# Order of the projections at the entry of a two-layer mixing stage: queries and keys by turns, and where their transposes, up projections and squares go

## The chip, the cores and the metric

The kernel runs on one core of one Trainium2 chip, in one launch. The metric is the device time of one execution in microseconds; for the kernel before it is the median of three runs. A core has a tensor engine (TensorE, PE in the profile; its weight loads are PEld), a vector engine (VectorE, DVE), a scalar engine (ScalarE, ACT), GpSimd (POOL) and SyncE (SP, which issues nearly all DMAs). Each engine works through its own instructions in order, and semaphores order them between engines.

## The reference

Two layers of a diffusion trunk, with 256 latent tokens and 256 context tokens of 1024 features. Each layer is a half-step gated feed-forward (FFN), a mixing stage and a second FFN; every sub-layer has an RMS norm with shift, scale and gate computed from the condition. The mixing stage projects the normalised tokens to five things and merges three groups of heads:

```python
q_lat, kv_lat, k_pe, sg_in, cv_in = jnp.split(hn @ w_mix_in[l], splits, axis=-1)
if last:   # layer 1: of the context only keys and values
    kv_lat_c, k_pe_c = jnp.split(hnc @ w_mix_in[l][:, OFF_KV:OFF_SG], [KV_LORA], axis=-1)
q = mla_queries(q_lat, g_q_lat[l], w_q_up[l], g_q_head[l], rope)
k, v = mla_keys_values(kv_lat, k_pe, g_kv_lat[l], w_kv_up[l], g_k_head[l], rope)
kc, vc = mla_keys_values(kv_lat_c, k_pe_c, g_kv_lat[l], w_kv_up[l], g_k_head[l], None)
attn = latent_attention(q, k, v, kc, vc)
sg = spatial_gating(sg_in, g_sgu[l], w_spatial[l], b_spatial[l])
cv = short_conv(cv_in, w_conv[l])
h = h + mod_l[5] * merge_groups(attn, sg, cv, g_out[l], w_mix_out[l])
```

Query latents have 384 columns, key and value latents 256 and the rotary part 32. Both are RMS-normalised, projected up to 8 heads, normalised again per head, and the rotary part is rotated. All is in float32.

## The kernel before

Every matrix product is three products of rounded halves: a weight block w is split into whi (rounded, by ScalarE, L124) and wlo (the rest, by VectorE or GpSimd, L125), the activations into xh and xl alike, and TensorE adds xh·whi, xl·whi and xh·wlo (`mm3` L393, `mm3x` L404 with the activations stationary).

The class `Weights` (L60) streams the weight blocks. SyncE loads them into six raw buffers, and at most five split blocks are held (`SUBB`). `pump(n)` issues the DMAs that have a buffer and splits up to n blocks that have a slot; with `W.hold` set, a plain pump splits none. `done(i)` gives a block's slot back in order. `W.low` names the engine of the low halves; the last job of an FFN sets it to GpSimd ("g", L627) and the next FFN's first job sets it to VectorE, so all low halves of a mixing stage are GpSimd's.

The program is a list of jobs, issued in order, and this order is the order of every engine's queue. TensorE's products go to six PSUM banks (`mm_bank`) and small ones to two (`sm_bank`).

At the border between two sub-layers a generator `chain` (L435) normalises the residual: squares summed by one-column products (`sums`), their inverse root (`rstd`), spread over the partitions by two products (`spread`), and then eight chunks, one per 128 features, each a VectorE multiplication (L364) into a scratch bank, a ScalarE rounding (L368) and a VectorE rest (L369). `step(c, n)` issues n such steps, `finish(c)` the rest. There is one chain for the latents (`c`) and one for the context (`cc`); both use the same two scratch banks in turn. The last block of an FFN (`out_last`) begins the latents' chain and prepares the first blocks of the mixing stage.

Mixing then runs, for layer 0 (`full`) and layer 1: `kv_lat` (L769), in which the steps of both chains alternate with the key products of the latents (288 columns) in three parts of 3, 3 and 2 k, and with half of the query products of the latents (384 columns); `kv_ctx` (L791), the keys of the context and the rest of the queries; in layer 0 `q_ctx`; `k_prep` (GpSimd's rotary tables); `uv_lat` (L869), the gate's products (512 columns), after which layer 1 transposes the normalised key and query latents (`kv_tr`, `q_tr`, L753) and normalises the gate (`v_norm`); six `conv_block`s with `spatial` behind the fourth; `y_sg`; `k_up` (L989); `y_cv_stats`; `q_up` (L1039); `y_cv`. Attention (`att`, L1229) runs the eight heads as a pipeline, beginning with the values' up projection (`v_up`). `mo_head`, `mo_block` and `mo_last` project the merged heads into the residual: `resid` (L410) adds a block (L415), squares it (L425) and adds the squares to a sum (L429), from which the next norm starts.

At the very start, `init` sums the squares of the input and `first_blocks` computes the first modulation (`ada0`, L1417) between the first FFN's products.

Of the kernel before, what the change touches and what calls it, by code (L numbers as in the profile page):

```python
# [173 lines left out]
def hybrid_trunk_kernel(ctx: ExitStack, tc: tile.TileContext, io: dict, out: bass.AP):  # L174
# [494 lines left out]
    def mixing(l):  # L669
# [99 lines left out]
        def kv_lat(W):  # L769
            c, cc = st.pop("lat_chain"), st.pop("ctx_chain")  # L770
            P["kvs"] = list(zip([W.take(), W.take(), W.take()], (3, 3, 2)))
            step(c, 2)
            b = [mm_bank(), mm_bank()]
            tok_part(b, P["kvs"][0:1], 0, 288, (0, 1))
            step(cc)
            step(c, 3)
            tok_part(b, P["kvs"][1:2], 3, 288, (0, 1))
            step(cc)
            finish(c)
            tok_part(b, P["kvs"][2:3], 6, 288, (0, 1))  # L780
            W.pump(2)
            step(cc, 3)
            qs = P["qs"] = [(W.take(), 2) for _ in range(2)]
            qb = P["qb"] = [mm_bank(), mm_bank()]
            tok_part(qb, qs, 0, 384, (0, 1))
            finish(cc)
            W.hold = False
            lat_evac(b, 256, "kvn0", (0, 1))
        job(kv_lat, kv_spec + q_spec[0:1])

        def kv_ctx(W):  # L791
# [5 lines left out]
            lat_evac(P["qb"], 384, "qn0")  # L797
            if not full:
                for (i, _, _), _ in P["qs"]:
                    W.done(i)  # L800
                preload(AF.Gelu_apprx_tanh)
        job(kv_ctx, q_spec[1:2])

# [65 lines left out]
        def uv_lat(W):  # L869
            P["uvs"] = [(W.take(), 2) for _ in range(4)]  # L870
            b = tok_mm(P["uvs"], 512, (0, 1), not full, W)
            uv_evac(b, (0, 1))
            if not full:
                kv_tr()
                q_tr()
                preload(AF.Sqrt)
                v_norm((0, 1), b)
        job(uv_lat, uv_spec)
# [110 lines left out]
        def k_up(W):  # L989
# [27 lines left out]
            last()  # L1017
            W.done(s)

        def v_up(W):  # L1020
# [18 lines left out]
        def q_up(W):  # L1039
            subs = [W.take() for _ in range(3)]  # L1040
            last = None
            for t in range(nq):
# [43 lines left out]
            last()  # L1086
            preload(AF.Exp)

        job(y_sg)
        job(k_up, ku_spec)  # L1090
        job(y_cv_stats)
        job(q_up, qu_spec)
        job(y_cv)
# [198 lines left out]
        sl = slice(0, NQ)  # L1292

        def mo_begin():
            j = len(P["mo"]) - 1
# [7 lines left out]
        def mo_head(W):  # L1303
# [15 lines left out]
            for j in range(3):  # L1319
                W.done(subs[j][0])  # L1320
                for s in halves():
                    resid(l, 5, j, banks[j], s, j == 0)
        job(mo_head)

        def mo_block(j):
            def fn(W):
# [4 lines left out]
                for hf in halves():  # L1331
                    resid(l, 5, j, bank, hf, False)
            return fn
# [3 lines left out]
        def mo_last(W):  # L1337
# [3 lines left out]
            for s, j in zip(subs, (6, 7)):  # L1341
                bl = mm_bank()
                mo_mm(bl, s, SC + AT, LAT, True, True)
                resid(l, 5, j, bl, LAT, False, last=not full and j == 7)
            if full:
# [27 lines left out]
    def init(W):  # L1373
# [25 lines left out]
        for i in range(40):  # L1399
            PE.matmul(bank[:, 128 * (i % 4):128 * (i % 4) + 128], lhsT=ones, rhs=ones, start=True, stop=True)  # L1400
        banks = [sums([acc[:, s]]) for s in (LAT, CTX)]
        st["init_rb"] = [(bank, rstd(bank, D)) for bank in banks]
    job(init)

    def first_blocks(in_spec, evac, half_mm):
# [5 lines left out]
        def ada0(W, j):  # L1411
            bank = sm_bank()
            for rnd in range(2):
# [23 lines left out]
        def fn(W):  # L1437
            rbs = st["acc"]
            W.pump(1)
            for s, (bank, r) in zip((LAT, CTX), st.pop("init_rb")):  # L1440
                ACT.activation(rbs[:, s], spread(bank, r), AF.Copy)
            bank = None
            sbs = {0: ada0(W, 0)}
            banks = [mm_bank() for _ in range(5)]
# [190 lines left out]
```

## Time and profile before

| | |
|---|---|
| median of three runs | 1722.94 us (1720.17 to 1725.0) |
| profiled execution | 1724.47 us, span 1722.7 us |
| PE, DVE, ACT, POOL busy | 97%, 66%, 39%, 14% |
| mean granted TensorE clock | 0.994 |
| DMA | 248.53 MB, mean 144 GB/s |

Times in the trace count from the start of the span. A busy TensorE share counts matmuls from start to end, and neighbours overlap; the rate of a dense stretch is read from the distance of their starts. The idle time of an engine is put down to what ended it. In the trace of this kernel layer 0's mixing stage begins at about 403 us and layer 1's at about 1370 us, and layer 1's attention at about 1451 us.

### The profile page before, as it was taken

Reading aid. Unit: us, or ns where it says so; the run is one execution under the profiler, and the core shown is the slowest. Engines: PE = TensorE matmul, PEld = TensorE weight load, DVE = VectorE, ACT = ScalarE, POOL = GpSimd, SP = SyncE. Lnnn points to the kernel's source line nnn. Section 1 sums busy time; section 2 is a strip of 40 time slices with the busy share of each in tenths; the row PEclk is TensorE's granted clock in tenths of the full one; section 3 lists DMA queues with packets and bytes.
Section 4 is the critical chain, followed back from the end, with each engine's and each line's share of the span. In section 5 each row is a group of like instructions: output and inputs, shape, how many; then the busy total and the mean of one; then the engine's idle time right before and its main releaser. Section 6 shows DMA issues by size and latency. Waiting matters only on the chain.

```text
span 1722.7 us, 23129 instructions
## 1 busy us (share of the span) xinstructions
PE 1678.1 (97%) x8858; PEld 1403.0 (81%) x8858; DVE 1140.6 (66%) x1868; ACT 668.8 (39%) x1139; POOL 246.0 (14%) x190
## 2 busy tenths in 40 slices
PE   8999999999999999999999999999999989899999
PEld 5788888888887788888878898888877877688887
DVE  5689988744257475777777447777776446577764
ACT  4422232224558543222322243322322266555552
POOL 0000000002447432000000030000000166630000
PEclk9999999999999999999999999999999999999999
DMA  8556566532321025555555325555554332146563
GB/s 310 184 184 190 190 189 191 163 105 81 95 86 50 20 92 155 164 169 162 162 167 162 119 88 159 171 171 170 156 166 147 88 115 94 50 159 190 182 189 89
DMA packets 71392, 248.53 MB, mean 144 GB/s; under 512 B 8048, under 2 KB 9584, under 8 KB 71280
## 3 DMA queue, kind: packets, MB, share of 16 engines
q1 hardware_dynamic: 71136, 246.97, 45.8%
q8 instruction: 70, 1.15, 0.3%
q14 instruction: 42, 0.34, 0.1%
q10 hardware_dynamic: 144, 0.07, 0.0%
HBM read 245.96 MB, written 1.05 MB: 143 GB/s over the span
## 4 chain that ended last, share of the span: by engine, by line
PE 89%; DVE 4%; POOL 2%; issue 2%; ACT 2%; DMA 1%; ACTq 0%; POOLq 0%; DVEq 0%
PE mm L394 23%; PE mm L395 23%; PE mm L396 22%; PE mm L401 7%; PE mm L402 4%; PE mm L405 2%; PE mm L407 2%; PE mm L406 2%; DVE acc L429 1%; POOL p L1168 1%; POOL wlo L125 1%; DVE mm L364 1%; DMA raw<-in_w_ada 1%; PE mm L1400 1%; PE mm L1188 1%
## 5 line engine op out<-in xcount | busy, mean ns | idle before, releaser
L124 ACT ACTIVATE whi<-raw 128x1024 fp32r<-128x1024 f32 (+1 forms) x334 | 340.0, 1022 | 606.8 <-PE mm L395 520.0
L394 PE MATMUL mm<-x,whi 128*128 128x512 f32 (+1 forms) x1360 | 508.4, 374 | 3.4 <-ACT x L366 2.0
L395 PE MATMUL mm<-x,whi 128*128 128x512 f32 (+1 forms) x1360 | 504.5, 371 | 2.2 <-DVE x L369 1.9
L396 PE MATMUL mm<-x,wlo 128*128 128x512 f32 (+1 forms) x1360 | 503.1, 370 | 0.5 <-DVE wlo L125 0.5
L125 DVE TENSOR_TENSOR wlo<-raw,whi 128x1024 fp32r<-128x1024 f32 (+2 forms) x257 | 304.4, 1187 | 237.1 <-ACT whi L124 236.9
L125 POOL TENSOR_TENSOR wlo<-raw,whi 128x1024 fp32r<-128x1024 f32 (+3 forms) x77 | 172.4, 2259 | 1205.0 <-ACT whi L124 1205.0
L269 DVE SCALAR_TENSOR_TENSOR scratch<-raw,cs,scratch 128x512 f32<-128x512 f32 x448 | 307.4, 745 | 0.0
L394 PEld LDWEIGHTS mm<-x,whi 128*128 128x128 f32 x1360 | 258.2, 190 | 51.3 <-issue 4.0
L395 PEld LDWEIGHTS mm<-x,whi 128*128 128x128 f32 x1360 | 258.3, 190 | 45.9 <-DVE x L369 3.8
L396 PEld LDWEIGHTS mm<-x,wlo 128*128 128x128 f32 x1360 | 258.3, 190 | 43.8 <-DVE wlo L125 0.9
L394 PE MATMUL mm<-g,whi 128*128 128x512 f32 (+1 forms) x594 | 220.9, 372 | 0.0
L396 PE MATMUL mm<-g,wlo 128*128 128x512 f32 (+1 forms) x594 | 219.4, 369 | 0.0
L395 PE MATMUL mm<-g,whi 128*128 128x512 f32 (+1 forms) x594 | 219.4, 369 | 0.0
L401 PE MATMUL mm<-x,whi 128*128 128x512 f32 x352 | 127.0, 405 | 1.8 <-DVE x L369 1.8
L395 PEld LDWEIGHTS mm<-g,whi 128*128 128x128 f32 x594 | 111.9, 188 | 20.6
L396 PEld LDWEIGHTS mm<-g,wlo 128*128 128x128 f32 x594 | 111.6, 188 | 20.9
L394 PEld LDWEIGHTS mm<-g,whi 128*128 128x128 f32 x594 | 111.7, 188 | 20.8
L487 ACT ACTIVATE g<-sa 128x512 fp32r<-128x512 f32 (+1 forms) x88 | 50.9, 579 | 130.1 <-DVE sa L478 119.3
L402 PE MATMUL mm<-x,wlo 128*128 128x256 f32 x352 | 100.0, 284 | 0.0
L488 DVE TENSOR_TENSOR g<-sa,g 128x512 fp32r<-128x512 f32 (+1 forms) x88 | 55.1, 626 | 56.8 <-ACT g L487 56.8
L401 PEld LDWEIGHTS mm<-x,whi 128*128 128x128 f32 x352 | 67.4, 192 | 18.9 <-DVE x L369 2.0
L402 PEld LDWEIGHTS mm<-x,wlo 128*128 128x128 f32 x352 | 67.9, 193 | 0.0
(218 smaller groups left out, 1777.1 us busy)
## 6 DMA issues: line engine op xcount, KB each, us to landing
raw<-in_w_ffn_in SPq DMA_DIRECT2D x176, 512.0 KB, 4.1
raw<-in_w_ada SPq DMA_DIRECT2D x144, 512.0 KB, 4.0
raw<-in_w_ffn_out SPq DMA_DIRECT2D x64, 512.0 KB, 3.6
raw<-in_w_ffn_out SPq DMA_DIRECT2D x32, 384.0 KB, 3.3
raw<-in_w_mo SPq DMA_DIRECT2D x16, 512.0 KB, 3.3
raw<-in_w_cv SPq DMA_DIRECT2D x12, 512.0 KB, 4.0
raw<-in_w_uv SPq DMA_DIRECT2D x8, 512.0 KB, 3.8
raw<-in_w_q SPq DMA_DIRECT2D x8, 384.0 KB, 3.1
```

What stands on the lines that cost most here:

```text
L124: nc.scalar.activation(hi[:, a:b], src, AF.Copy)
L125: eng.tensor_tensor(lo[:, a:b], src, hi[:, a:b].bitcast(F32), ALU.subtract)
L269: DVE.scalar_tensor_tensor(acc[:, s], src, cv, acc[:, s], ALU.mult, ALU.add)
L394: PE.matmul(bank, lhsT=wh, rhs=xh, start=first, stop=False)
L395: PE.matmul(bank, lhsT=wh, rhs=xl, start=False, stop=False)
L396: PE.matmul(bank, lhsT=wl, rhs=xh, start=False, stop=last)
L401: PE.matmul(bank, lhsT=wh, rhs=x2, start=first, stop=False, skip_group_check=True)
L402: PE.matmul(bank[:, 256:512], lhsT=wl, rhs=x2[:, 0], start=False, stop=last, skip_group_check=True)
L405: PE.matmul(bank, lhsT=xh, rhs=wh, start=first, stop=False)
L406: PE.matmul(bank, lhsT=xh, rhs=wl, start=False, stop=False)
L487: ACT.activation(st["gh"][:, m, 0:n], sa[:, 0:n], AF.Copy)
L488: DVE.tensor_tensor(st["gl"][:, m, 0:n], sa[:, 0:n], st["gh"][:, m, 0:n].bitcast(F32), ALU.subtract)
```

## The change

In layer 0 (`full`) `kv_lat` interleaves: the latents' keys come in the same three parts, but a quarter of the query products stands ahead of the second and of the third. In layer 1 a new job `q_kv_lat` does all latent queries first, between the chains' steps, then the latents' keys; `kv_last` does the context's keys. Layer 1's `uv_lat` issues `kv_tr` after half of the gate's products and `q_tr` after three quarters, and its query up projection is issued ahead of the key's. In layer 1's output projection, and for the last two latent blocks of layer 0's, the squares go to the free half of the block's own PSUM bank (`room`) and not to an SBUF buffer. At the start the sums, their roots and the first modulation products come first, and then the spread and the first weight split.

```diff
@@ kv_lat
-            step(c, 3)
+            step(c, 1)
+            W.pump(1)
+            step(c, 2)
+            qs = P["qs"] = [(W.take(), 2)]
+            qb = P["qb"] = [mm_bank(), mm_bank()]
+            tok_part(qb, qs, 0, 384, (0, 1))
             tok_part(b, P["kvs"][1:2], 3, 288, (0, 1))
             step(cc)
+            W.pump(1)
             finish(c)
+            qs.append((W.take(), 2))
+            tok_part(qb, qs[1:2], 2, 384, (0, 1))
             tok_part(b, P["kvs"][2:3], 6, 288, (0, 1))
-            W.pump(2)
             step(cc, 3)
-            qs = P["qs"] = [(W.take(), 2) for _ in range(2)]
-            qb = P["qb"] = [mm_bank(), mm_bank()]
-            tok_part(qb, qs, 0, 384, (0, 1))
             finish(cc)
             W.hold = False
             lat_evac(b, 256, "kvn0", (0, 1))
-        job(kv_lat, kv_spec + q_spec[0:1])
+
+        def q_kv_lat(W):
+
+            c, cc = st.pop("lat_chain"), st.pop("ctx_chain")
+            qb = [mm_bank(), mm_bank()]
+            qs = [(W.take(), 2) for _ in range(3)]
+            step(c, 2)
+            tok_part(qb, qs[0:1], 0, 384, (0, 1), W)
+            step(cc)
+            step(c, 2)
+            W.pump(1)
+            tok_part(qb, qs[1:2], 2, 384, (0, 1), W)
+            step(cc)
+            finish(c)
+            W.pump(1)
+            qs.append((W.take(), 2))
+            tok_part(qb, qs[2:3], 4, 384, (0, 1), W)
+            step(cc, 3)
+            W.pump(1)
+            tok_part(qb, qs[3:4], 6, 384, (0, 1), W)
+            W.pump(1)
+            finish(cc)
+            W.hold = False
+            P["kvs"] = list(zip([W.take(), W.take(), W.take()], (3, 3, 2)))
+            lat_evac(qb, 384, "qn0")
+            b = tok_mm(P["kvs"], 288, (0, 1), False, W)
+            lat_evac(b, 256, "kvn0", (0, 1))
+
+        def kv_last(W):
+            b = tok_mm(P["kvs"], 288, (2, 3), True, W)
+            lat_evac(b, 256, "kvn1", (2, 3))
+            preload(AF.Gelu_apprx_tanh)
+        if full:
+            job(kv_lat, kv_spec + q_spec[0:1])
+        else:
+            job(q_kv_lat, q_spec + kv_spec)
@@ uv_lat, layer 1
+            b = [mm_bank(), mm_bank()]
+            tok_part(b, P["uvs"][0:2], 0, 512, (0, 1), W)
+            kv_tr()
+            tok_part(b, P["uvs"][2:3], 4, 512, (0, 1), W)
+            q_tr()
+            tok_part(b, P["uvs"][3:4], 6, 512, (0, 1), W)
             uv_evac(b, (0, 1))
-            if not full:
-                kv_tr()
-                q_tr()
-                preload(AF.Sqrt)
-                v_norm((0, 1), b)
+            preload(AF.Sqrt)
+            v_norm((0, 1), b)
@@ q_up, and the order of the up projections
             subs = [W.take() for _ in range(3)]
+            W.hold = True
...
+        ups = [(k_up, ku_spec), (q_up, qu_spec)]
         job(y_sg)
-        job(k_up, ku_spec)
+        job(*ups[not full])
         job(y_cv_stats)
-        job(q_up, qu_spec)
+        job(*ups[full])
         job(y_cv)
@@ output projection
+        def sq_room(bank):
+
+            return None if full else bank[:, 256:512]
...
-                    resid(l, 5, j, bank, hf, False)
+                    resid(l, 5, j, bank, hf, False, room=sq_room(bank))
...
-                resid(l, 5, j, bl, LAT, False, last=not full and j == 7)
+                last = not full and j == 7
+                resid(l, 5, j, bl, LAT, False, last=last, room=None if last else bl[:, 256:512])
@@ start
+            stats = [(s, sums([rbs[:, s]])) for s in (LAT, CTX)]
+            rs = [rstd(bank, D) for s, bank in stats]
+            sbs = {0: ada0(W, 0)}
+            for (s, bank), r in zip(stats, rs):
+                ACT.activation(rbs[:, s], spread(bank, r), AF.Copy)
+            bank = stats = None
             W.pump(1)
-            for s, (bank, r) in zip((LAT, CTX), st.pop("init_rb")):
-                ACT.activation(rbs[:, s], spread(bank, r), AF.Copy)
-            bank = None
-            sbs = {0: ada0(W, 0)}
```

Left out: the preloads of ScalarE's tables, which move with the jobs that need them (Exp to the end of `k_up` in layer 1), `kv_ctx`, which is layer 0's alone now, and the first `ada0`, which takes an `mm_bank` as both small banks hold the sums.

## Rows read from the trace of the kernel before

**Rows 1.** The page, part 1: busy time, share of the span and instructions by engine.
```profile
PE 1678.1 (97%) x8858; PEld 1403.0 (81%) x8858; DVE 1140.6 (66%) x1868; ACT 668.8 (39%) x1139; POOL 246.0 (14%) x190
```

**Rows 2.** Waits of PE: who waited for whom; us in total, times, longest.
```profile
PE mm L1188 <- POOL p L1168: 6.0, 11, 0.7
PE mm L407 <- DVE x L369: 4.4, 4, 1.2
PE sm L1417 <- DMA raw<-in_w_ada: 3.8, 3, 1.9
PE mm L405 <- DVE x L369: 3.3, 2, 1.7
PE mm L753 <- DVE kvl L756: 2.2, 1, 2.2
...
PE sm L320 <- DVE acc L429: 1.9, 2, 1.5
...
PE mm L406 <- POOL wlo L125: 1.4, 1, 1.4
```

**Rows 3.** Timeline of PE, layer 1's first projections: start, us, engine line op, xcount, [idle before].
```profile
1369.79 0.30 PE L405 MATMUL mm<-whi,x 128*128 128x288 f32 x1
...
1370.58 0.29 PE L405 MATMUL mm<-whi,x 128*128 128x288 f32 x1
...
1372.25 0.40 PE L407 MATMUL mm<-whi,x 128*128 128x288 f32 x1 [1.24 <-DVE x L369]
...
1379.88 0.34 PE L405 MATMUL mm<-whi,x 128*128 128x384 f32 x1
...
1383.87 0.34 PE L407 MATMUL mm<-whi,x 128*128 128x384 f32 x1
```

**Rows 4.** Timeline of PE, from layer 1's gate products to its first conv product.
```profile
1396.75 0.39 PE L405 MATMUL mm<-whi,x 128*128 128x512 f32 x1
...
1409.39 1.47 PE L753 MATMUL mm<-ident,k_tok 128*128 128x128 f32 x12
...
1413.72 0.39 PE L394 MATMUL mm<-x,whi 128*128 128x256 f32 x1 [0.22 <-DVE kvl L756]
```

**Rows 5.** Timeline of DVE, two neighbouring chunks of layer 1's chain.
```profile
1375.60 0.49 DVE L364 SCALAR_TENSOR_TENSOR mm<-h,amod,sm 128x256 f32<-128x256 f32 x1
...
1376.51 0.49 DVE L364 SCALAR_TENSOR_TENSOR mm<-h,amod,sm 128x256 f32<-128x256 f32 x1
```

**Rows 6.** The page, part 5: groups of instructions; busy us, mean ns | idle before.
```profile
L124 ACT ACTIVATE whi<-raw 128x1024 fp32r<-128x1024 f32 (+1 forms) x334 | 340.0, 1022 | 606.8 <-PE mm L395 520.0
```

**Rows 7.** Waits of POOL from 1385 to 1440 us: total, times, longest.
```profile
POOL wlo L125 <- ACT whi L124: 22.5, 3, 14.2
```

**Rows 8.** Timeline of POOL, layer 1's conv blocks.
```profile
1422.61 2.42 POOL L125 TENSOR_TENSOR wlo<-raw,whi 128x1024 fp32r<-128x1024 f32 x1 [3.38 <-ACT whi L124]
```

**Rows 9.** Timeline of PE, the first head of layer 1's attention.
```profile
1453.30 0.31 PE L1113 MATMUL mm<-ident,q_tok 128*96 128x128 f32 x1 [1.77 <-POOL q_tok L1080]
```

**Rows 10.** Timeline of POOL and DVE: a sum of squares from PSUM, one from SBUF.
```profile
1370.12 3.62 POOL L125 TENSOR_TENSOR wlo<-raw,whi 128x768 fp32r<-128x768 f32 x2 [3.01 <-ACT whi L124]
...
1370.99 0.42 DVE L429 TENSOR_TENSOR acc<-acc,mm 128x256 f32<-128x256 f32 x1 [0.52 <-ACT mm L425]
...
1523.21 1.57 DVE L429 TENSOR_TENSOR acc<-acc,sq 128x256 f32<-128x256 f32 x1 [0.54 <-ACT sq L425]
```

**Rows 11.** Windows: length, busy us by engine, granted clock (PEclk), DMA share, GB/s.
```profile
30.00:35.00 5.00, 5.00 (x23) 3.36 (x21) 1.25 (x2) 0.84 (x2) 0.00 (x0) 0.67 0.99 356
...
1500.00:1510.00 10.00, 8.85 (x48) 8.43 (x49) 3.46 (x9) 4.33 (x8) 4.47 (x4) 0.66 0.16 52
```

**Rows 12.** Timeline of DVE and PE at the start.
```profile
14.72 1.23 DVE L125 TENSOR_TENSOR wlo<-raw,whi 128x1024 fp32r<-128x1024 f32 x1 [0.85 <-ACT whi L124]
15.01 1.07 PE L1417 MATMUL sm<-raw,cs 128*32 128x256 f32 x16 [0.66 <-ACT acc L1441]
...
17.06 0.17 DVE L1432 TENSOR_REDUCE mods<-sm 128x4 f32<-128x16 f32 x1 [1.12 <-PE sm L1427]
```

More of the change, by code (lines that the diff above doesn't have):

```diff
@@ L797, in kv_ctx @@
             lat_evac(P["qb"], 384, "qn0")
-            if not full:
[L799 to L802, printed above, removed]
+        if full:
+            job(kv_ctx, q_spec[1:2])
+        else:
+            job(kv_last)
         if full:
@@ L870, in uv_lat @@
             P["uvs"] = [(W.take(), 2) for _ in range(4)]
-            b = tok_mm(P["uvs"], 512, (0, 1), not full, W)
-            uv_evac(b, (0, 1))
-            if not full:
-                kv_tr()
-                q_tr()
-                preload(AF.Sqrt)
-                v_norm((0, 1), b)
+            if full:
+                b = tok_mm(P["uvs"], 512, (0, 1), False, W)
+                uv_evac(b, (0, 1))
+                return
+            b = [mm_bank(), mm_bank()]
[4 more added lines that the diff above has]
+            tok_part(b, P["uvs"][3:4], 6, 512, (0, 1), W)
+            uv_evac(b, (0, 1))
+            preload(AF.Sqrt)
+            v_norm((0, 1), b)
         job(uv_lat, uv_spec)
@@ L1018, in k_up @@
             W.done(s)
+            if not full:
+                preload(AF.Exp)
         def v_up(W):
@@ L1086, in q_up @@
             last()
-            preload(AF.Exp)
+            if full:
+                preload(AF.Exp)
+        ups = [(k_up, ku_spec), (q_up, qu_spec)]
         job(y_sg)
-        job(k_up, ku_spec)
+        job(*ups[not full])
         job(y_cv_stats)
-        job(q_up, qu_spec)
+        job(*ups[full])
         job(y_cv)
@@ L1321, in mo_head @@
                 for s in halves():
-                    resid(l, 5, j, banks[j], s, j == 0)
+                    resid(l, 5, j, banks[j], s, j == 0, room=sq_room(banks[j]))
         job(mo_head)
@@ L1400, in init @@
             PE.matmul(bank[:, 128 * (i % 4):128 * (i % 4) + 128], lhsT=ones, rhs=ones, start=True, stop=True)
-        banks = [sums([acc[:, s]]) for s in (LAT, CTX)]
-        st["init_rb"] = [(bank, rstd(bank, D)) for bank in banks]
     job(init)
@@ L1411, in ada0 @@
         def ada0(W, j):
-            bank = sm_bank()
+            bank = sm_bank() if j else mm_bank()
             for rnd in range(2):
```

## The prediction

> **What bounds the kernel now.** Read first the engine line of the page: TensorE is busy 97% of the span [rows 1], so a change can win little more than the 44.6 us in which it sits idle, and it wins only where a wait goes that nothing later replaces. Then read who ends TensorE's waits [rows 2]. Four waits of 4.4 us in all end on the low half of a normalised chunk of x (VectorE L369) ahead of L407, two of 3.3 us on the same line ahead of L405; they are two alike sets (1.24, 0.95, 1.67 us), one in each layer, where the mixing stage begins. The 2.2 us wait behind the transposes' eviction, the 1.4 us wait for a low half of weights and the 1.9 us for the squares' sum are layer 1's alone or nearly so. The timeline then shows where they lie [rows 3, 4, 9].
>
> In layer 1 the stretch from the first key product (1369.79) to the first gate product (1396.75) takes 26.96 us [rows 3, 4]. Its products: a key product starts 0.132 us after the last (1369.79 to 1370.58, six of them), a query product 0.1735 us after it (1379.88 to 1383.87, 23 steps) [rows 3]. There are 96 key products (two times 8 k, 2 tiles, 3 terms) and 48 query products: 12.7 + 8.3 = 21.0 us. So 6.0 us are waits, statistics and products that follow the chunks. The chunks come every 0.91 us (1375.60 to 1376.51) [rows 5], while six key products give only 0.79 us of work for each: keys alone can't cover the chain. Six query products give 1.04 us.
>
> **Layer 1, queries first (q_kv_lat, kv_last).** The first wait stays but for 0.25 us, since the second chunk is as late as before (1372.25) and six query products cover 1.04 us instead of 0.79. From there 1.04 us of products stand against 0.91 us of chain, so the second wait goes. After the queries come the keys of the latents, which need no new x and take two banks that the residual freed long before; only then the context's keys, which need the chain's two scratch banks. Queries and latent keys end at about 1369.8 + 1.1 + 8.3 + 6.3 + 0.6 (sums, spread) = 1386.1. The added W.pump calls put four conversions into ScalarE's queue in front of chunks: 1.02 us for each of the two of 1024 columns [rows 6], by their columns 0.86 and 0.57 us for the keys' 864 and 576. Half of that finds ScalarE idle; the rest may bring the last chunk, now at 1386.4, to about 1387; that leaves a wait of some 0.5 us where 1.67 stood (half of the 3.3 us in rows 2). New stretch: 21.0 + 1.1 + 0.6 + 0.5 = 23.2, against 26.96: 3.8 us less. Bounds: 1.5 (the conversions delay every chunk) to 4.9 (only the first wait is left).
>
> **Gate products with the transposes in between (uv_lat).** From 1396.75 to 1413.72 is 16.97 us [rows 4]. The 48 products need 12.64 - 1.42 = 11.2 us (1396.75 to 1409.39 less the wait for a low half), 14 transposes 1.5 us (12 took 1.47). The 1.42 us wait goes, as the first two low halves of the gate's weights are now made by GpSimd during the chain, where it idles for most of 14.2 us [rows 7], and not after it. The 2.20 us wait goes too: kv_tr's banks are evicted during the next 2.8 us of products, and q_tr finds them free. New: 12.7 us; 4.2 us less. Bounds: 2.2 (the low halves still come late) to 4.3.
>
> **Queries up ahead of keys up.** The first head's transposes wait 1.77 us for GpSimd's rotation of the queries [rows 9]. With queries first this rotation lies beside 24 products of k_up, of the gate products' width and so 5.6 us (11.2 / 48 each). What is late next is the last key tile, which VectorE and GpSimd must finish while v_up's 24 products run, another 5.6 us. 1.8 us less; bounds 0.8, if that tile is late, to 1.8. W.hold moves with the first of the two; in both orders five halves are prepared ahead, so attention prepares the same weights.
>
> **Squares in PSUM (resid's room).** In layer 1's output projection the sum acc + sq takes 1.57 us [rows 10] where the one that reads its squares from PSUM takes 0.42, with GpSimd at work beside both (1370.12 for 3.62 us). All but the last are covered by the next block's products; the last holds back the residual and the sums for the next norm, and TensorE waits. 1.1 us less; bounds 0.4 to 1.2.
>
> **What these lean on.** Everything after conv begins is 8 us earlier, and GpSimd must follow: of its waits in 1385 to 1440 us, 22.5 us in all, 14.2 are the first and 3.38 the last, before 1422.61 [rows 7, 8]. Two low halves of 2.4 us that move ahead and this pause are 8.2 us, just enough. The pause is ScalarE's, which has the gate's norm ahead of the next conversion; in the new order by my count this norm still ends about 10 us after the gate's last product. So small waits for low halves before the fifth conv block and in the queries' up projection are likely: I put 0.8 us on them, between 0 and 4. Sum of layer 1: 3.8 + 4.2 + 1.8 + 1.1 - 0.8 = 10.1 us less.
>
> **Layer 0, the same by turns (kv_lat).** Keys stay first, and queries now fill the gap of the second wait. But all six banks are taken (two of scratch, two of keys, two of queries), so the context's keys must still wait for the last chunks. The products ahead of this wait are the same ones, and its end is set by the chain: filling the gaps only lengthens the last wait from 1.67 to about 3.5 us. The chain's context half starts behind twelve more query products: 2.1 us, less the 0.95 us wait that they fill and 0.4 us by which chunks held up three k of keys. Of these 0.8 us VectorE, itself still at the last latent chunks, hides the most: +0.2 us, bounds 0 to 0.8. The pump calls there find all five slots held and do nothing.
>
> A long idle stretch has a price of its own. Between 25 and 30 us TensorE has its longest wait but one (1.90 us), and from 30 to 35 us the granted clock averages 0.67: it fell from the upper level, 2.4 GHz, to 1.2 for two thirds of 5 us; from 1500 to 1510 us, where the output projection takes over from attention, it is 0.66 [rows 11]. Dense products then lose half of that time, 1.65 and 3.4 us. For the new 3.5 us wait I take 1.2 us, nearest to the first of these rows less what falls into the wait; bounds 0 to 3.4. Layer 0: +1.4 us.
>
> **Start.** The first modulation products (15.01, 1.07 us) now run right behind the sums, about 1.5 us earlier, and so do the DMA requests that they release; TensorE's three waits for such transfers, 3.8 us, are ahead [rows 2, 12]. But the first weight conversion moves behind the spread, and its low half (1.23 us at 14.72) then ends near 17.9 on VectorE, ahead of the reduction that ran at 17.06 [rows 12]: the first chunk is 0.85 us late. I take -0.2 us, nearest to nothing, as the next transfer but two decides; bounds -1.3 to +0.9. The rest of the change in layer 0 (squares of the last two latent blocks in PSUM) meets no slow sum there and costs nothing.
>
> **Sum.** -10.1 + 1.4 - 0.2 = -8.9 us on the profiled execution's 1724.47 (span 1722.7 and 1.8 around it): 1715.6. That run lies 1.5 us above the median of the three runs, 1722.94; on the median it gives 1714.0, my forecast, with 1709.5 to 1717 as this case's own range.
>
> **Rivals.**
> *GpSimd becomes the bound.* If its pause stays whole (3.4 us) and one more low half (1.2 us of it) is late, the gain at the up projections shrinks by 4.0 in place of 0.8: 1717.2. For it: in the 17 us after that second wait it has none. Against: two low halves are really moved ahead. Chance 0.15.
> *The clock falls in layer 0 for long.* If TensorE comes out of its 3.5 us wait as it worked from 1500 to 1510 us, the fall costs 3.4 us and not 1.2: 1716.2 [rows 11]. For it: no wait now is as long. Against: behind the 1.90 us wait it fell for half as long. Chance 0.10. The Trainium skill, page "TensorE: Matmul & The Clock Gate", section "HAM oscillation — how this bites in real kernels", says in other words that a long gap ahead of dense products is paid twice, since TensorE comes back at half clock; the 0.67 after 30 us agrees.
> *Attention takes the gain back.* It waits 6.0 us in eleven waits for GpSimd's scaling of probabilities [rows 2]; if something with its own due time (the four weight blocks prepared there) set its pace, layer 1 would keep the 1.1 us of squares and a third of the other 9.0: -1.1 - 3.0 + 1.4 - 0.2 = -2.9 us, 1720.0. Against: these preparations are issued from the heads' own steps, which move with it. Chance 0.06.
> *Slower: a bank wait in layer 1.* If the latent keys get the banks of the queries instead of those of the residual, they wait for lat_evac of the queries, which stands behind the whole context chain on ScalarE: from 1380 until about 1389.5, 9.5 us, and 1.65 us of clock behind it. -8.9 + 9.5 + 1.65 = +2.2: 1725.1. It decides once the wait exceeds 7.3 us. For it: the 1.67 us wait is of this kind. Against: banks seem to come back in the order of release, and the residual's were released first. Chance 0.06.
>
> **Chances.** The forecast's case has 0.63. About 0.3% (5.2 us) is what a measurement of this kernel can tell from no change: faster means below 1717.8. The first case lies under that but for 0.03, the two mild rivals for three quarters and nine tenths, the others not: 0.60 + 0.11 + 0.09 = 0.80 faster. Slower by as much needs the bank wait half as long again, half of its case: 0.03. Within: 0.17. Range 1709.5 to 1719: it leaves out a tenth below and the attention and bank cases above.
>
> **What would show it.** Right: in layer 1 the first gate product about 24 us after the first query product, no wait ahead of L753, the first head's transposes right behind v_up, all layer 1 sums on L429 near 0.42 us; in layer 0 one wait of 3 us or more ahead of the context's keys. Wrong: waits of L396 or L406 for low halves above 2 us in all, a wait inside layer 1's latent keys, or an entry of layer 0 that is shorter than before.

## The result, and the profile after

The changed kernel took 1708.95 us (median of four runs, 1707.53 to 1711.08), the kernel before 1721.56 us (four runs, 1718.73 to 1725.0): a ratio of 0.9925, interval 0.9908 to 0.9942, or 12.9 us less with an interval of 10.0 to 15.8. Forecast were 8.9 us less and 1714.0 us; 1708.95 lies 0.55 us below the range. The sign and the places were right, the size was not. The profiled execution of the changed kernel took 1711.08 us (span 1709.3), 13.4 us less than the 1724.47 of before.

TensorE works as long as before, and is idle for 32.4 us instead of 44.6 [rows 1]:

```profile
PE 1676.9 (98%) x8858; PEld 1403.9 (82%) x8858; DVE 1131.3 (66%) x1868; ACT 667.7 (39%) x1139; POOL 245.6 (14%) x190
```

Its waits in the same view as [rows 2] (us in total, times, longest):

```profile
PE mm L1237 <- POOL p L1217: 4.7, 8, 0.7
PE sm L1469 <- DMA raw<-in_w_ada: 4.3, 4, 1.5
PE mm L405 <- DVE x L369: 3.4, 1, 3.4
PE mm L407 <- DVE x L369: 2.1, 2, 1.2
...
PE sm L320 <- ACT sq L425: 0.9, 1, 0.9
...
PE mm L396 <- POOL wlo L125: 0.2, 1, 0.2
```

The three chunk waits of layer 1 have become one of 0.87 us. The waits for the low half and for the transposes' banks are gone but for 0.2 us, and at the end of the output projection TensorE waits 0.9 us for the last squares, where it waited 2.0 us for the sum and for them. Layer 0 has the one wait of 3.4 us that was forecast. The timeline of TensorE in layer 1 answers [rows 3, 4, 9] (start, us, instructions, idle before):

```profile
1370.33 0.34 PE L405 MATMUL mm<-whi,x 128*128 128x384 f32 x1
...
1372.79 0.44 PE L407 MATMUL mm<-whi,x 128*128 128x384 f32 x1 [0.87 <-DVE x L369]
...
1393.47 0.39 PE L405 MATMUL mm<-whi,x 128*128 128x512 f32 x1
...
1398.94 0.60 PE L753 MATMUL mm<-ident,k_tok 128*128 128x128 f32 x4
...
1402.56 0.82 PE L753 MATMUL mm<-ident,k_tok 128*128 128x128 f32 x6
...
1405.97 0.28 PE L394 MATMUL mm<-x,whi 128*128 128x256 f32 x1
...
1443.84 0.38 PE L1162 MATMUL mm<-ident,q_tok 128*96 128x128 f32 x2
1444.05 0.60 PE L1162 MATMUL sm<-ident,k_tok 128*96 128x128 f32 x4
```

First query to first gate product 23.14 us (26.96 before, 23.2 forecast); gate products with the transposes inside 12.50 (16.97 before, 12.7 forecast); the first head's transposes follow v_up without a wait. The sums on L429 in the output projection, 1.57 us before [rows 10], take 0.42 us, as forecast (shortest, median and longest in ns, first and last start; the first of the seven read PSUM before too):

```profile
L429 DVE TENSOR_TENSOR acc<-acc,mm x7: 420/421/422, 1371.5 to 1509.6; 128x256 f32<-128x256 f32 x7
```

What was not forecast shows in the windows (length, busy us by engine, granted clock, DMA share, GB/s), here of the falls of TensorE's clock from 2.4 to 1.2 GHz in the changed kernel, with the start of its output projection, the sixth row:

```profile
19.70:23.20 3.50, 3.50 (x12) 2.19 (x16) 1.70 (x4) 1.13 (x2) 0.00 (x0) 0.51 0.84 279
405.40:408.90 3.50, 3.50 (x13) 3.50 (x13) 3.02 (x8) 1.68 (x4) 0.00 (x0) 0.51 0.71 218
419.00:422.60 3.60, 3.60 (x16) 3.53 (x17) 1.49 (x4) 1.07 (x7) 0.00 (x0) 0.53 0.00 0
589.70:593.20 3.50, 3.38 (x9) 2.64 (x9) 3.10 (x8) 2.14 (x6) 1.97 (x3) 0.51 0.00 0
1453.30:1456.80 3.50, 3.50 (x13) 2.79 (x12) 1.44 (x3) 2.71 (x7) 3.50 (x4) 0.51 0.36 89
1491.00:1501.00 10.00, 8.90 (x73) 8.56 (x71) 4.90 (x12) 7.25 (x12) 7.47 (x5) 1.00 0.19 56
1514.70:1521.70 7.00, 5.61 (x17) 4.81 (x18) 6.32 (x16) 4.10 (x11) 0.00 (x0) 0.51 0.03 14
```

Before, the output projection's first products ran at 0.66 of the full clock [rows 11]; here at 1.00, with the same waits ahead. The fall that stood near 30 us before stands near 20 us here. So part of the 13.4 us between these two executions is the clock's, and the question became whether that part belongs to the change.

The stretches of the two executions by first products, in us, add up to the span. "start" ends at layer 0's first key product, "L0" at its latents' transposes, "entry" runs from layer 1's first projection to its gate products, "gate" from there to the first conv product, "conv" to the transposes of the spatial gate's output (`y_sg`), "ups" from these to the first head's key transposes, "out" from the first output product that waits for the norm to the last feed-forward stage:

```
                 start    L0   to L1  entry  gate  conv   ups  attention   out    rest
before          403.32  35.31  931.16  26.96 16.98 18.71 21.02    48.14  27.73  193.37
changed         400.94  38.47  930.92  23.14 12.50 19.03 19.06    48.12  23.92  193.20
difference       -2.38  +3.16   -0.24  -3.82 -4.48 +0.32 -1.96    -0.02  -3.81   -0.17
```

Three terms are far from the forecast: the start (-0.2 forecast), layer 0 (+1.4) and the output projection (-1.1).

### The profile page after: what moved, and what is told of

It is laid out like the page before. It is cut to its first block, busy times and chain, and to the rows that moved or that the text cites. A ratio compares the mean times of both kernels' runs of the same rounds, so it can differ in the third digit from the quotient of the medians.

```text
span 1709.3 us, 23126 instructions
## 1 busy us (share of the span) xinstructions
PE 1676.9 (98%) x8858; PEld 1403.9 (82%) x8858; DVE 1131.3 (66%) x1868; ACT 667.7 (39%) x1139; POOL 245.6 (14%) x190
## 4 chain that ended last, share of the span: by engine, by line
PE 93%; DVE 3%; POOL 1%; ACT 1%; issue 1%; DMA 0%; ACTq 0%; POOLq 0%; DVEq 0%
PE mm L394 23%; PE mm L395 23%; PE mm L396 23%; PE mm L401 7%; PE mm L402 4%; PE mm L405 3%; PE mm L407 3%; PE mm L406 3%; POOL p L1217 1%; DVE acc L429 1%; PE mm L1237 1%; PE mm L1454 1%; PE sm L1260 1%; PE sm L320 1%; POOL wlo L125 0%
## 5 line engine op out<-in xcount | busy, mean ns | idle before, releaser
L124 ACT ACTIVATE whi<-raw 128x1024 fp32r<-128x1024 f32 (+2 forms) x334 | 340.4, 1022 | 609.3 <-PE mm L395 515.4
L125 DVE TENSOR_TENSOR wlo<-raw,whi 128x1024 fp32r<-128x1024 f32 (+1 forms) x257 | 304.1, 1186 | 238.8 <-ACT whi L124 238.8
L125 POOL TENSOR_TENSOR wlo<-raw,whi 128x1024 fp32r<-128x1024 f32 (+4 forms) x77 | 172.2, 2258 | 1196.1 <-ACT whi L124 1196.1
```

What stands on the lines that cost most here:

```text
L124: nc.scalar.activation(hi[:, a:b], src, AF.Copy)
L125: eng.tensor_tensor(lo[:, a:b], src, hi[:, a:b].bitcast(F32), ALU.subtract)
```

## The experiments

Executions of one kernel spread over up to 9 us (the kernel before: 1718.0 to 1726.8 in 29 runs), so each part was timed beside the kernel before (at every ratio below, the kernel before is the base), and its stretches read from its own profiled execution, which also gives further samples of every stretch that it leaves alone.

### The start alone

```
+ stats = [(s, sums([rbs[:, s]])) for s in (LAT, CTX)]
+ rs = [rstd(bank, D) for s, bank in stats]
+ sbs = {0: ada0(W, 0)}              # ahead of the spread
...
  W.pump(1)                          # now behind it
```

> The kernel before with the changed start alone (the sums, the first modulation products ahead of the spread, the first weight conversion behind it). Theory A (the terms that the two traces show): 2.4 us less than before, all of it ahead of 35 us, the clock's first fall near 20 us instead of 30 us, nothing else moved but by the shift. Theory B (the terms of the prediction): 0.2 us less, and the 2.4 us between the two traces came from something else. If the fall of the clock at 1501 to 1508 us depends on where the schedule stands in time, this kernel, 2.4 us earlier, may lose it or move it, worth up to another 3 us; if it belongs to what runs there, it stays.

Measured: 1720.16 us beside 1722.11, ratio 0.9992 (0.9981 to 1.0003). The start took 401.91 us. Its two requests for weights that wait for a free buffer leave at 13.89 us, 14.05 in the full change, and 15.97 in the kernel before (start, us, engine line op):

```profile
13.89 0.80 SPq L102 DMA_DIRECT2D raw<-in_w_ffn_in  x2
```

Over all profiled executions the old start took 402.6 to 405.0 us (eight, mean 403.7), the new one 400.9 to 402.6 (four, mean 401.8): 1.9 us less, nearer to theory A's 2.4 than to theory B's 0.2, though the timing alone does not tell it from nothing. The fall at the output projection stayed (1504 us).

The profiles show where the gain lies. In the kernel before, TensorE waits at the start for the norm and the first conversion too, and in the changed kernel (second block) less of that is left (the view of [rows 2]):

```profile
PE mm L394 <- ACT x L368: 1.1, 1, 1.1
...
PE sm L1417 <- ACT acc L1441: 0.7, 1, 0.7
...
PE sm L1427 <- ACT sa L1421: 0.5, 1, 0.5
PE mm L396 <- DVE wlo L125: 0.5, 1, 0.5
```

```profile
PE mm L394 <- ACT x L368: 0.4, 1, 0.4
PE sm L1479 <- ACT acc L1495: 0.3, 1, 0.3
```

Between 12 and 60 us all waits for ScalarE and VectorE come to 3.0 us before and 0.7 us after (2.2 to 3.9 us in the eight executions of the old start, 0.3 to 1.0 us in the four of the new), while the waits for transfers of `w_ada` grew from 3.8 to 4.3 us in this pair. So the earlier requests did not shorten the waits for transfers there; the waits for ScalarE's and VectorE's work are what went.

Not foreseen by either theory: layer 1, untouched here, was 3 us longer than in the first execution of before, with two falls of the clock that this one did not have:

```profile
1374.50:1381.30 6.80, 6.03 (x25) 5.67 (x25) 4.88 (x12) 2.46 (x6) 0.00 (x0) 0.50 0.47 149
1415.40:1418.90 3.50, 3.50 (x17) 3.50 (x18) 2.07 (x7) 2.30 (x5) 3.50 (x2) 0.51 0.60 174
```

### Half of the start

```
  W.pump(1)                          # as before, ahead of the spread
+ stats = [(s, sums([rbs[:, s]])) for s in (LAT, CTX)]
+ rs = [rstd(bank, D) for s, bank in stats]
+ sbs = {0: ada0(W, 0)}              # ahead of the spread
```

> The kernel before with one half of the changed start: the first modulation products ahead of the norm's spread, but the first weight conversion still ahead of it. The other kernels give the start (span's start to the first key product of layer 0) as 403.8 us on average with the old start (eight executions, 402.6 to 405.0) and 401.9 us with the new one (four, 400.9 to 402.6). Theory F (the gain comes from the two weight requests that wait for the modulation's buffers and now leave at 14.1 us instead of 16.0): the requests leave by 14.5 us here too and layer 0 begins at 401 to 403 us. Theory G (it is the later conversion, which lets VectorE and ScalarE finish the norm first): the requests leave early, but layer 0 begins at 403 to 405 us as with the old start. One execution can differ by 1 us, so only a clear value tells.

Measured: 1720.84 us beside 1721.95, ratio 0.9992 (0.9980 to 1.0004). The requests left at 15.97 us, as before, although the modulation products that were to release them ended at 14.9 us; the low half of the first conversion ended at 15.95 us in both kernels, which fits requests that wait for the conversion's buffer. Yet layer 0 began at 401.11 us; but this was the one execution in which the clock did not fall at all in the start:

```profile
12.00:34.00 22.00, 16.13 (x123) 9.80 (x123) 13.70 (x32) 9.70 (x19) 0.00 (x0) 1.00 0.95 340
```

It fits neither theory. TensorE's waits for ScalarE and VectorE between 12 and 60 us came to 2.5 us here, so by this execution most of what the whole edit takes from them needs the later conversion too; but which half of the start gives the 1.9 us stays open.

### Layer 0 alone

```
+ def kv_lat_turns(W):   # the new kv_lat
...
- job(kv_lat, kv_spec + q_spec[0:1])
+ job(kv_lat_turns if full else kv_lat, kv_spec + q_spec[0:1])
```

> The kernel before with layer 0's key and query latents by turns alone. Theory A: 3.2 us more than before up to the first transposes of the latents in layer 0 (1.8 us by the chain of the context, 1.3 us by half-speed products behind one wait of 3.4 us), falls of the clock near 405 and 419 us in the trace's time moved by 2.4 us. Theory B (the prediction's terms): 0.2 us by the chain and 1.2 us by the clock, 1.4 us more. Without the fall near 405 us the chain's part should be the smaller one, some 0.5 us.

Measured: 1723.25 us beside 1722.11, ratio 1.0007 (0.9995 to 1.0019), 1.2 us more. The wait is the forecast one, and the clock falls behind it (timeline, then window):

```profile
419.59 0.61 PE L405 MATMUL mm<-whi,x 128*128 128x288 f32 x1 [3.41 <-DVE x L369]
```

```profile
405.00:419.00 14.00, 10.51 (x70) 10.18 (x70) 11.63 (x28) 6.49 (x15) 2.12 (x2) 1.00 0.30 89
419.50:423.00 3.50, 3.41 (x14) 3.41 (x15) 1.56 (x5) 1.30 (x8) 0.00 (x0) 0.51 0.00 0
```

From the first key product (403.22) to this wait's end it is 16.37 us, 16.10 before (403.32 to 419.42): 0.27 by the chain, where 0.2 was forecast. The fall adds 1.2 (20.43 us from there to the transposes, 19.21 before), where 1.2 was forecast. The 3.2 us of theory A need a second fall, at 405 us as in the profile after: A had taken one execution's clock for the change's. But a fall is not the new order's alone. In three of the eleven executions with the old order (start_only at 418.8 us, gate_only at 421.2, fill_out at 419.4) the clock fell behind the old wait of 1.67 us as well, and L0 took 36.83 to 36.85 us there instead of 35.30 to 35.33; with one fall the new order took 36.80. So 1.2 to 1.5 us is what a fall costs here. That the new order has one more often (two executions of two) is likely, but two executions don't show it.

### Layer 0 undone

```
- tok_part(qb, qs, 0, 384, (0, 1))   # the turns of kv_lat
+ (kv_lat of the kernel before)
```

> The changed kernel with layer 0's key and query latents in the old order again. Theory A: 3.2 us less than the changed kernel, some 1705.8 us by the medians, no wait of 3 us in layer 0, falls of the clock near 405 and 419 us gone; since everything behind stands 3.2 us earlier, a fall may move into the output projection of layer 1 again, which would give back up to 3 us. Theory B: 1.4 us less than the changed kernel, 1707.5 us.

Measured: 1707.46 us beside 1722.11, ratio 0.9914 (0.9898 to 0.9930); L0 took 35.30 us and the falls of 405 and 419 us were gone. That is 1.5 us under the changed kernel's median, what theory B says, though the two intervals overlap. No fall came into the output projection. The kernel of the last experiment has the same layer 0 and had a fall at 419 us, so one execution without it is a draw too.

### The squares alone

```
- resid(l, 5, j, banks[j], s, j == 0)
+ resid(l, 5, j, banks[j], s, j == 0, room=sq_room(banks[j]))
```

> The kernel before with the squares of the output projection of layer 1 (and the last two latent blocks of layer 0) in PSUM alone. Up to 1500 us nothing changes. Theory A (the fall of the clock at 1501 to 1508 us is set by what stands ahead of it and by time): the fall stays, the wait for the last sum goes, 1.3 us less than before. Theory C (the squares edit itself keeps the clock up, as it takes VectorE and GpSimd work from beside the products): no fall between 1500 and 1510 us, 3.8 us less than before. The prediction's term: 1.1 us less.

Measured: 1721.02 us beside 1722.11, ratio 0.9992 (0.9982 to 1.0002). The wait for the sum went, and the fall at the output projection stayed (third row), so theory C falls. The entry and conv, untouched, again had falls (first two rows):

```profile
1373.20:1380.00 6.80, 6.04 (x26) 5.68 (x26) 4.80 (x12) 2.39 (x6) 0.00 (x0) 0.50 0.48 154
1414.20:1417.70 3.50, 3.50 (x17) 3.50 (x18) 2.07 (x7) 2.27 (x5) 3.50 (x2) 0.51 0.65 181
1503.00:1509.80 6.80, 6.33 (x28) 6.16 (x29) 1.99 (x5) 2.56 (x5) 3.84 (x3) 0.50 0.04 5
```

"out" took 26.47 us with that fall. Without one the old form took 25.2 us (25.21, 25.31, 25.19 in three executions) and the new form 23.92 in the full change: 1.3 us for the squares.

A new theory followed. D: a wait of TensorE is paid twice, as idle time and in some executions again as products at half clock behind it; the waits that the change removes had this second price too, and the execution of before that the forecast was made on happened not to show it in the entry and conv. E: falls come whatever TensorE does there.

### Layer 1 alone

The changed kernel, less its two edits outside layer 1:

```
- sbs = {0: ada0(W, 0)}              # first_blocks, and init, as before
...
- tok_part(qb, qs, 0, 384, (0, 1))   # kv_lat as before
```

> The changed kernel with the start and layer 0's mixing as before: all of layer 1's edits and nothing else. Theory D: the two falls of layer 1's entry go with the waits, so that the difference to before is 11 to 13 us (a ratio of 0.9925 to 0.9936) and the entry takes 23.1 us, the conv 19.0 us. Theory B (the prediction's terms for layer 1, no price of the clock behind the waits that go): 10.1 us less, a ratio of 0.9941.

Measured: 1710.81 us beside 1722.43, ratio 0.9932 (0.9915 to 0.9948), 11.7 us less; entry 23.15, conv 19.02 us, no fall in either. It lies on theory D's side, but 0.9941 is inside the interval.

### The entry alone, the gate alone

The first diff is that of the entry alone, the second that of the gate alone:

```
- job(kv_lat, kv_spec + q_spec[0:1])
+ if full:
+     job(kv_lat, kv_spec + q_spec[0:1])
+ else:
+     job(q_kv_lat, q_spec + kv_spec)
```

```
+ tok_part(b, P["uvs"][0:2], 0, 512, (0, 1), W)
+ kv_tr()
+ tok_part(b, P["uvs"][2:3], 4, 512, (0, 1), W)
+ q_tr()
+ tok_part(b, P["uvs"][3:4], 6, 512, (0, 1), W)
```

> The kernel before with queries first in layer 1's entry alone. Both theories: the entry takes 23.1 us. Theory D: the fall that followed the entry's waits (1374 or 1389 us) is gone, the one behind the waits of 1.4 and 2.2 us ahead of conv (1414 to 1416 us) stays, conv 20.2 us where it falls; about 5 us less than before. Theory B: 3.8 us less. GpSimd may be late with the gate's low halves as before; then the 1.4 us wait stays.

> The kernel before with layer 1's transposes within the gate's products alone. Theory D: the 2.2 us wait goes, and with it the fall at 1414 to 1416 us if the 1.4 us wait for a low half, which this edit does not touch, is not enough for it; the entry's fall (28.4 us instead of 27) stays in most executions; 2.2 to 4 us less than before. Theory B: 2.4 us less, no change at conv.

Measured: entry alone 0.9974 (0.9963 to 0.9986), gate alone 0.9974 (0.9960 to 0.9988), each 4.5 us less. With the new entry (23.15 us, no fall) the 1.4 us wait for the gate's low half went too, and the 2.2 us wait stayed, with a fall right behind it; with the new gate this wait went and there was no fall, though the 1.42 us wait stayed. Neither timing tells theory D from B. In the stretches, the entry alone gives -3.82 and -1.73 us (the gate), the gate alone -2.75 us and +0.32 (conv) beside executions without a fall. The two waits that stayed, each followed by a window behind it, are first those of the entry alone, then those of the gate alone:

```profile
1409.16 0.44 PE L753 MATMUL mm<-ident,k_tok 128*128 128x128 f32 x2 [2.20 <-DVE kvl L756]
```

```profile
1410.20:1413.70 3.50, 3.50 (x19) 3.50 (x19) 2.04 (x7) 1.98 (x4) 0.00 (x0) 0.51 0.62 207
```

```profile
1403.53 0.50 PE L406 MATMUL mm<-wlo,x 128*128 128x512 f32 x1 [1.42 <-POOL wlo L125]
```

```profile
1404.00:1416.00 12.00, 12.00 (x73) 10.50 (x72) 4.46 (x6) 10.07 (x25) 11.84 (x14) 1.00 0.51 154
```

### Queries up first alone

```
- job(k_up, ku_spec)
+ job(*ups[not full])
...
- job(q_up, qu_spec)
+ job(*ups[full])
```

> The kernel before with layer 1's queries up ahead of its keys up alone. Both theories: the stretch from the gate's last transposes to the first head's key transposes takes 19.1 us instead of 21.0, 1.9 us less than before (the prediction's term was 1.8). If instead the queries' rotation is late for another reason, the wait of 1.8 us stays. Falls of the clock in layer 1's entry and ahead of conv as in the kernel before, in some executions and not in others.

Measured: 1720.9 us beside 1723.11, ratio 0.9985 (0.9974 to 0.9997), 2.6 us less; "ups" took 19.06 us. The first head's transposes directly follow v_up:

```profile
1452.89 0.38 PE L1118 MATMUL mm<-ident,q_tok 128*96 128x128 f32 x2
1453.11 0.60 PE L1118 MATMUL sm<-ident,k_tok 128*96 128x128 f32 x4
```

### Layer 1's waits filled with work

```
+ def fill(bank, n, w):
+     for i in range(n):
+         PE.matmul(bank, lhsT=w[:, 0:128], rhs=w[:, 0:512], start=True, stop=True)
...
+ if k in fills:
+     fill(*fills[k], wh)
```

> The kernel before, its order kept; in layer 1 alone 31 spare products of 512 columns (0.23 us each, their results are not used) stand ahead of the five points where TensorE waited: 5, 4, 7 ahead of the three waits for chunks (1.24, 0.95, 1.67 us), 6 ahead of the low half (1.42), 9 ahead of the last transposes (2.20). Theory D (a wait there is paid twice, once as idle time and again as products at 1.2 GHz behind it): no fall between 1365 and 1440 us, the stretch from the first key product of layer 1 to the first gate product about 27 us instead of the 28.4 that three of four executions of this order showed, conv (first product to the transposes of the gate) 18.7 us instead of 20.2, and a median 1 to 3 us less than before although TensorE has 7.1 us more work. Theory E (falls come at times of their own, whatever TensorE does): the falls stay in the same places in most executions, and the time is that of before or up to 1 us more.

Measured: 1722.38 us beside 1722.43, ratio 1.0004 (0.9994 to 1.0014). No fall between 1365 and 1440 us, entry 26.98 and conv 18.72 us, at no cost of the 31 products; but the time did not fall, which speaks for E. It decides little: other executions of the old order (gate_only, ups_only, start_mod) had no fall in the entry either, without any filling.

### Waits filled that no part of the change touches

```
+ fill(1 if full else 2)
  rbs = [spread(bank, r) for bank, r in zip(sbs, rs)]
+ fill(4)
...
+ fill(3)
  step(c)
+ fill(2)
  step(c)
...
+ fill(7, ba)
```

> The changed kernel with layer 0's mixing in the old order, and spare products of 512 columns (0.23 us each, their results are not used) in waits that no part of the change touches: ahead of the norm's spread and of the first product of the output projection in both layers (1 and 4 in layer 0, 2 and 4 in layer 1), and at the entry of layer 1's last feed-forward stage 3 ahead of the sums (wait 0.91 us), 2 ahead of the spread (0.55) and 7 ahead of the first product (1.77). In all ten executions read so far the clock fell at two of these places (near 586 to 592 us once, at the last entry once or twice). Theory D (a wait is paid a second time by the clock): these falls go, 1.4 us at the first place and 1.5 to 3 us at the second, together 3 to 4.5 us less than the same kernel without them (ratio to the kernel before 0.989 instead of 0.9914). Theory E (the falls do not depend on whether TensorE works in the wait): the falls stay, the ratio stays at 0.9914 or up to 0.0005 above it.

Measured: 1705.28 us beside 1723.11, ratio 0.9902 (0.9883 to 0.9920), the lowest median here. The windows of the kernel without the spare products (587.7 and 1512.8 us) and with them:

```profile
587.70:591.20 3.50, 3.46 (x8) 2.78 (x9) 2.94 (x7) 2.15 (x7) 2.12 (x3) 0.51 0.00 0
1512.80:1519.70 6.90, 5.74 (x18) 4.89 (x19) 6.22 (x15) 3.99 (x11) 0.00 (x0) 0.51 0.02 10
```

```profile
586.00:596.00 10.00, 9.66 (x48) 7.52 (x48) 5.36 (x14) 5.17 (x12) 4.38 (x5) 1.00 0.01 2
1506.00:1520.00 14.00, 13.65 (x81) 10.70 (x79) 8.15 (x20) 5.80 (x13) 4.30 (x2) 1.00 0.39 127
```

Both falls, present in every one of the other twelve executions, are gone. The first is worth 1.4 us: from layer 0's first head to layer 1's first projection 844.37 us, 845.77 in the kernel without the spare products, 845.7 to 846.5 in all others. At the second the stage from there to the end took 191.98 us, against 193.20 and 193.46 in the two executions with the same layer 1 and the same pace of products (the last section has the two paces): 1.2 to 1.5 us. So theory E falls at these two places, as far as one execution with spare products can show: there the clock did not fall where TensorE worked through the wait. The Trainium skill, page "TensorE: Matmul & The Clock Gate", section "HAM oscillation — how this bites in real kernels", says that a wait ahead of the products throttles them and advises to shape the loop so that TensorE stays busy; this trace agrees, with 0.51 turned into 1.00. A wait does not always bring a fall: ahead of layer 1's output projection the same wait of 1.0 us stands in the twelve other executions, and the clock fell at it in six. By medians the gain over the kernel without spare products is 2.2 us, less than the 3 to 4.5 expected, and the two intervals overlap, so the timing alone does not show a gain.

## Why the prediction was right in its places and wrong in size

- **Layer 1, queries first** (-3.8 forecast): -3.82 in executions without a fall. One wait of 0.87 us is left; the 0.5 us that was allowed for the last chunk did not come.
- **Gate and transposes** (-4.2): -4.48, the same in all four executions that have both edits. Entry and gate alone show who pays for what: the 1.4 us wait goes with the entry, as GpSimd is then early, the 2.2 us wait with the transposes.
- **Queries up first** (-1.8): -1.96. **Squares** (-1.1): -1.3. **New small waits** (+0.8): conv +0.32, of which one wait of 0.15; GpSimd, named as the rival that would become the bound, kept up.
- Without falls layer 1 gives -3.82 - 4.48 + 0.32 - 1.96 - 1.3 = -11.2 where -10.1 was forecast. This sum is 1.1 us larger: the allowance for small waits took 0.5 us of it, the gate 0.3, and the up projections and the squares 0.2 each. Attention gave nothing back (-0.02), and no bank wait came into the latent keys: both of these rivals fell.
- **Layer 0** (+1.4): +0.27 and +1.2 alone, +1.2 by its timing (between -0.9 and +3.3). The chain's part is right, and so is the cost of one fall; that it got one fall and not two or none is partly luck, as the old order has one there at times, and the profile after had two. The rival with a longer fall fits the profile after only in that a second fall came at 405 us.
- **Start** (-0.2, bounds -1.3 to +0.9): -1.9 by the means over twelve executions. This is the step that failed most. I had looked for the gain in the waits for transfers, put it near nothing, "as the next transfer but two decides", and counted the later conversion as a loss of 0.85 us. The transfer part was rightly small: TensorE's waits for them grew, 3.8 to 4.3 us. What I left out of the sum is that TensorE also waits at the start for ScalarE's and VectorE's norm and first conversion, 3.0 us in all, and that the new order takes 2.3 us of this away. The first chunk was 0.44 us later in this pair of profiles (first product at 19.67, 19.23 before); over all executions it was not late (19.2 to 21.0 us with the old start, 19.5 to 20.0 with the new). Part of the means' difference may be the clock's: by the granted clock the old start had 9.4 us at half speed on average and the new 6.0, and where it had most, 10 to 14 us in five executions, TensorE waited only 1.3 to 2.3 us for transfers. But with a single fall in either the new start took 400.94 us and the old 403.22 and 403.32. How much is the clock's, and how the two edits share the rest, is open.
- **The clock behind the waits that go** was priced at nothing, though I priced it behind the wait that comes. The execution forecast on had no fall in the entry or ahead of conv; others of the same order had. Entry: 28.40, 28.51, 28.41 us with a fall, 26.95 to 26.99 without (four). Conv behind the 2.2 us wait: 20.07 to 20.22 with (four), 18.70 or 18.71 without (three). The new order had none in five and four executions. The means of the old order lie 0.6 and 0.8 us above the fall-free ones, and "out" (25.2 without, 26.5 to 27.8 with, five of eight) 1.3 us.

Together: -11.2 for layer 1, -1.9 for the start, +1.2 for layer 0 make -11.9. The 12.9 of the ratio leaves 1.0 us to the clock. Of the 4.0 us by which the forecast of -8.9 fell short, the start thus has 1.7, layer 1 has 1.1, the clock 1.0 and layer 0 has 0.2. The clock's 1.0 is less than the 2.7 that these means would allow, and both are inside the interval of 2.9 us either way. That the entry's and conv's falls go for good is plausible but not shown: the old entry had one in three executions of seven, the new in none of five, and filling the same waits gained nothing measurable. "out" still has the wait ahead of it, and its fall came in none of the three executions with all of layer 1's edits and nothing in this wait, and in six of the nine others, so its share may be the luck of the profiled executions. It also matters what the forecast was measured from: 1722.94 was the median of three runs, 1721.56 that of the four beside the result, 1.4 us of the 5.05 by which the time was missed.

## What to carry to other kernels

One profiled execution is one draw of the clock: before a stretch's length is used as a term, look whether a fall lies in it, and price the clock behind the waits that go as well as behind those that come. In a kernel whose TensorE is 97% busy, reordering work that is there anyway, so that each wait finds other products ready, was worth eight times the edit that shortens a side engine's instruction (10.3 to 1.3 us). Where a wait can't be filled with real work, spare products in it cost nothing that could be measured here, and in the one execution of each of the two kernels that had them no fall followed a filled wait; that they make a kernel faster is not shown (ratios 1.0004, and 0.9902 beside 0.9914).

## What the runs showed of the hardware that was not expected

The places of the falls differ between executions with the same schedule, also far from any edit: in the old entry of layer 1 the clock fell at 1374 us in start_only and 1373 us in sq_only, at 1389 us in l0_only, and not at all in four others. Together with the two paces below, this is what was found to differ in stretches that no edit touches.

The products of the last feed-forward stage have two paces at a granted clock of 1.00. In the execution of the changed kernel and in the one with layer 0 undone, the same products in windows of 80 us (count, busy us, mean ns):

```profile
L401 PE MATMUL mm<-x,whi 128*128 128x512 f32 x227 | 80.3, 399 | 0.0
L402 PE MATMUL mm<-x,wlo 128*128 128x256 f32 x228 | 64.0, 281 | 0.0
```

```profile
L401 PE MATMUL mm<-x,whi 128*128 128x512 f32 x232 | 80.5, 391 | 0.0
L402 PE MATMUL mm<-x,wlo 128*128 128x256 f32 x231 | 64.7, 280 | 0.0
```

Here 232 products fit where 227 did. The slower pace costs the stage 2.2 us (193.20 us to the end in the one execution, 190.98 in the other, the same fall in both); other kernels with this stage unchanged showed the one or the other, and what selects it is not known. From the start of a product of 512 columns to that of the 256-column one behind it the median is 235 or 236 ns in seven of the thirteen executions, both profiles of before and after among them, and 230 to 231.5 ns in six.
